# A decoder block on one core: sums of h2 from stored fp32 blocks with grouped plain tiles, and the second MLP product in passes (2,4), (3,5), (1,6), 7

## The chip, the core and the metric

The kernel runs on one core of a Trainium2 chip. Its time is device time in microseconds (us) for one execution. The engines are TensorE (PE; PEld are its weight loads), VectorE (DVE), ScalarE (ACT), GpSimd (POOL) and SyncE (SP, which here only issues DMAs). Each engine works through its own instructions in the order in which they stand in its queue. Names as L1018 are lines of the kernel before.

## The reference

The block has sequence 1024, width 1024 and one layer, all in fp32: a normalisation, two kinds of attention with a gated merge, an output projection, and then the MLP and a last normalisation. The change lies in this last part:

```
h2 = rmsnorm(x, g_norm2) * (1 + scale2) + shift2
x  = x + gate2 * (square(relu(h2 @ w_mlp1)) @ w_mlp2)     # 1024 x 4096, then 4096 x 1024
return rmsnorm(x, g_final)
```

## The kernel before

**Precision.** Every fp32 operand of a matmul is split into a high half (an fp32r copy, by ScalarE) and a low half (the operand less the high half, mostly by VectorE), and a product takes three matmuls: high x high, high x low, low x high.

**h2.** The output projection's rows are normalised into `xn2` (L813), transposed by TensorE into banks (L824), scaled by ScalarE into an fp32 tile `hf2` (L826, a ring of three), and split by VectorE and GpSimd into the `big` tiles `h2[g]` (L828, L829): g is the half of the sequence, k the block of 128 channels.

**First product.** It gives 32 tiles f of 128 hidden units, for two halves of the sequence. Tiles 0 to 3 are plain (`plain_tiles`, L882: 24 matmuls for each tile and half); the other 28 go in 14 pairs through a seven-product scheme of the Strassen-Winograd kind (`pair`, L928, `prod`, L915: 12 matmuls each). The scheme needs four combinations of h2's quarters, T1 to T4 (`combos`, L892), which are made from the split halves between plain tiles 0, 1 and plain tiles 2, 3 (L971). `finish` (L846) applies relu and square and keeps tiles ("hold", "cc") until the four members of a group J of four tiles are there; GpSimd then makes the sums that a second, Strassen, scheme needs on its left side, and they are stored to DRAM as `U_d[1]` to `U_d[7]`.

**Second product.** It runs over eight J (512 hidden units each) in four passes: the Strassen products (2,6), (3,5), (1,4) and 7. In a pass of two, eight banks of PSUM hold 4 tiles of each product, and a unit of 24 matmuls adds one J to four banks (`accumulate`, L1022). A unit's operands are prepared by `operands` (L1013): a block of U_d and one of `w_mlp2`, or a sum of two of its blocks made by GpSimd (L1033), are loaded through the ring `raw` (L995, the first seven in memory of the weight pools, then 20 buffers), and ScalarE and VectorE split them into one of four tiles `ut` of 16 KB a partition. After each pass the banks are added into 16 tiles `C` (rows r, columns c, t). In pass 7 the first four J come bank after bank, the last four J finish one bank at a time.

**The end.** In pass 7 all rows are finished (L1121): x is loaded from `X_d`, C is multiplied by the gate (`g2b`, L1126), GpSimd adds (L1127), ScalarE squares with a sum (L1103), and `output` (L1105) makes the reciprocal root, the scalings and the stores.

**Memory and order.** Memory is a stack of pools on each side; tiles of a pool lie one behind the other in the order in which they are first asked for, and a tile waits for what lay there before. Left of the second product's pools lie only constants and weight buffers (32 KB); above these lay the 64 KB of `big` tiles. The order on each engine is set by a planner that simulates the program: of the instructions that are ready, the one that stands first in the program goes first; semaphores are added afterwards.

## Time and profile before

| | us |
|---|---|
| median of 3 runs | 1708.5 (1706.05 to 1708.88) |
| the profiled execution | 1707.44 |
| its span | 1705.6 |
| TensorE busy | 1592.6 (93%) |
| VectorE busy | 1179.3 (69%) |
| ScalarE busy | 958.0 (56%) |
| GpSimd busy | 736.0 (43%) |
| mean granted TensorE clock | 0.963 |

The span runs from the first to the last instruction that the profile shows. Busy shares are means over the whole span; stages differ. Matmuls are pipelined, so that their shown durations overlap: the pace of a stage is its length over its matmuls.

### The profile page before, as it was taken

Reading aid. Unit: us, or ns where it says so; the run is one execution under the profiler, and the core shown is the slowest. Engines: PE = TensorE matmul, PEld = TensorE weight load, DVE = VectorE, ACT = ScalarE, POOL = GpSimd, SP = SyncE. Lnnn points to the kernel's source line nnn. Section 1 sums busy time; section 2 is a strip of 40 time slices with the busy share of each in tenths; the row PEclk is TensorE's granted clock in tenths of the full one; section 3 lists DMA queues with packets and bytes.
Section 4 is the critical chain, followed back from the end, with each engine's and each line's share of the span. In section 5 each row is a group of like instructions: output and inputs, shape, how many; then the busy total and the mean of one; then the engine's idle time right before and its main releaser. Section 6 shows DMA issues by size and latency. Waiting matters only on the chain. (4 is left out here: it accounts for less than half of the span.)

```text
span 1705.6 us, 22762 instructions
## 1 busy us (share of the span) xinstructions
PE 1592.6 (93%) x7585; PEld 1315.8 (77%) x7585; DVE 1179.3 (69%) x2271; ACT 958.0 (56%) x1678; POOL 736.0 (43%) x611
## 2 busy tenths in 40 slices
PE   5989999998989999999999998699999889999986
PEld 3768787787778888888887887488888668888875
DVE  6786999989945556566767358866555377658478
ACT  4466897896666777666742154355445343434343
POOL 3421112131114565666532117776667543245472
PEclk8999999998999999999999999799999989999998
DMA  9221122121323444545956331254344597566832
GB/s 303 73 47 57 42 72 60 50 71 44 91 51 101 124 128 107 162 146 152 337 175 234 119 116 50 93 167 161 136 153 144 191 364 247 195 239 213 278 100 99
DMA packets 215997, 242.53 MB, mean 142 GB/s; under 512 B 48432, under 2 KB 133504, under 8 KB 215880
## 3 DMA queue, kind: packets, MB, share of 16 engines
q1 hardware_dynamic: 208968, 226.39, 42.3%
q10 hardware_dynamic: 6912, 14.68, 2.2%
q8 instruction: 60, 0.98, 0.2%
q14 instruction: 57, 0.47, 0.1%
HBM read 180.19 MB, written 60.84 MB: 141 GB/s over the span
## 5 line engine op out<-in xcount | busy, mean ns | idle before, releaser
L75 PE MATMUL g<-h_hi,whi 128*128 128x512 f32 x656 | 267.5, 408 | 8.2 <-DVE KA L313 5.8
L75 PE MATMUL g<-h_hi,wlo 128*128 128x512 f32 x656 | 264.9, 404 | 0.0
L75 PE MATMUL g<-h_lo,whi 128*128 128x512 f32 x656 | 263.8, 402 | 0.0
L117 POOL TENSOR_TENSOR wlo<-st,whi 128x1024 fp32r<-128x1024 f32 x56 | 136.9, 2446 | 292.4 <-ACT whi L116 227.9
L1019 DVE TENSOR_TENSOR ut<-rw,ut 128x1024 fp32r<-128x1024 f32 x112 | 186.3, 1706 | 96.5 <-ACT ut L1018 96.5
L1018 ACT ACTIVATE ut<-rw 128x1024 fp32r<-128x1024 f32 x112 | 112.1, 1052 | 154.3 <-PE pv L75 71.5
L1033 POOL TENSOR_TENSOR rw<-rw 128x1024 f32<-128x1024 f32 x40 | 107.9, 2697 | 152.0 <-DMA rw<-in_w_mlp_dram 139.5
L75 PEld LDWEIGHTS g<-h_hi,whi 128*128 128x128 f32 x656 | 126.7, 193 | 34.3 <-DVE KA L313 3.6
L75 PEld LDWEIGHTS g<-h_hi,wlo 128*128 128x128 f32 x656 | 126.2, 192 | 25.0
L75 PEld LDWEIGHTS g<-h_lo,whi 128*128 128x128 f32 x656 | 126.6, 193 | 23.9
L75 PE MATMUL S<-ut 128*128 128x512 f32 (+1 forms) x576 | 139.1, 387 | 4.9 <-DVE C L1074 4.9
L75 PEld LDWEIGHTS S<-ut 128*128 128x128 f32 x576 | 107.8, 193 | 27.0 <-DVE C L1074 5.3
L572 ACT ACTIVATE ph<-ptr 128x512 fp32r<-128x512 f32 (+1 forms) x160 | 86.1, 551 | 56.8 <-PE ptr L571 52.7
L573 DVE TENSOR_TENSOR pl<-ptr,ph 128x512 fp32r<-128x512 f32 (+1 forms) x160 | 99.5, 630 | 26.4 <-ACT ph L572 22.6
L75 PE MATMUL g<-ut 128*128 128x512 f32 (+1 forms) x384 | 96.8, 389 | 20.5 <-ACT ut L1018 12.8
L116 ACT ACTIVATE whi<-st 128x1024 fp32r<-128x1024 f32 x72 | 75.8, 1053 | 71.1 <-PE g L75 23.1
L555 ACT ACTIVATE sp<-sp,mn 128x128 f32<-128x128 f32 (+7 forms) x128 | 98.5, 771 | 28.8 <-DVE mn L551 28.5
L486 DVE TENSOR_SCALAR_CACHE_REDUCE bjunk<-sel_all,cand 128x384 bf16<-128x384 int16 (+7 forms) x132 | 106.5, 806 | 1.4
L558 ACT ACTIVATE sp<-sp,mn 128x128 f32<-128x128 f32 (+7 forms) x128 | 96.8, 770 | 18.7 <-DVE mn L557 18.2
L571 PE MATMUL ptr<-ident,sp 128*128 128x128 f32 x576 | 91.8, 276 | 9.6 <-DVE pl L573 9.6
L75 PEld LDWEIGHTS g<-ut 128*128 128x128 f32 x384 | 71.5, 195 | 35.8 <-ACT ut L1018 13.2
L75 PE MATMUL pv<-ph,V 128*128 128x256 f32 x320 | 87.3, 292 | 1.6 <-DVE yt L580 0.9
(420 smaller groups left out, 3975.5 us busy)
## 6 DMA issues: line engine op xcount, KB each, us to landing
...
```

The source lines that it names most:

```text
L75: nc.tensor.matmul(o, l, r, start=start, stop=stop)
L116: nc.scalar.activation(hi, st, AF.Copy)
L117: (lo_eng or nc.vector).tensor_tensor(lo, st, hi.bitcast(F32), op=ALU.subtract)
L486: nc.vector.tensor_scalar(bjunk[:, :(i + 1) * P], sel[i].bitcast(dt), thr[:, q], None, op0=ALU.is_ge, op1=ALU.add, accum_out=cnt[:, q])
L555: nc.scalar.activation(sp[:, :W], sp[:, :W], AF.Exp, bias=mn[:, len(cs) - 1:len(cs)], scale=-1.0, accum_out=mn[:, 2:3])
L558: nc.scalar.activation(sp[:, :W], sp[:, :W], AF.Copy, scale=mn[:, 3:4])
L571: nc.tensor.transpose(tr[:, n * P:(n + 1) * P], pt[s][:, kb * P:(kb + 1) * P], ident)
L572: nc.scalar.activation(ph[:, z:], tr[:, z:], AF.Copy)
L573: nc.vector.tensor_tensor(pl[:, z:], tr[:, z:], ph[:, z:].bitcast(F32), op=ALU.subtract)
L1018: nc.scalar.activation(ut[:, n], t, AF.Copy)
L1019: nc.vector.tensor_tensor(ut[:, n + 1], t, ut[:, n].bitcast(F32), op=ALU.subtract)
L1033: nc.gpsimd.tensor_tensor(o, a, b, op=op)
```

## The change

Each `hf2` block is also stored in DRAM (`H_d`), its low half is always made by VectorE, and the ring has four tiles. All four plain tiles are one group, first half before second half of the sequence for all four; the weights of tiles 2 and 3 lie in the memory of T4. The holds of group 0 lie in the rings "u" and "cc". T1 to T4 are made after that in the program from the stored fp32 blocks, loaded back through SP: one VectorE difference each, then the split; T4's split comes last. The four `ut` tiles get a pool of their own that is made before all others of the second product. The passes are (2,4), (3,5), (1,6), 7, so that C of rows 4 to 7, columns 0 is final after the first and C of rows 0 to 3, columns 1 after the second; their residuals (`residual`) are made in J = 1 to 4 of the next pass. In pass 7 VectorE makes all residual sums; the outputs of rows 4 to 7 are stored by SP, those of rows 0 to 3 by ScalarE and SP.

```
+H_d = drm.tile([2, KT, P, 512], F32, name="H_d")
...
-                        hf2 = pO.tile([P, 512], F32, name="hf2", tag="hf2", bufs=3)
+                        hf2 = pO.tile([P, 512], F32, name="hf2", tag="hf2", bufs=4)
                         nc.scalar.activation(hf2, tp, AF.Identity, scale=ab[:, 2, k:k + 1], bias=ab[:, 3, k:k + 1])
                         hh, hl = [h2[g][v][k // 4][:, k % 4, :] for v in range(2)]
                         nc.vector.tensor_copy(hh, hf2)
-                        (nc.gpsimd if k % 2 else nc.vector).tensor_tensor(hl, hf2, hh.bitcast(F32), op=ALU.subtract)
+                        nc.vector.tensor_tensor(hl, hf2, hh.bitcast(F32), op=ALU.subtract)
+                        nc.sync.dma_start(H_d[g, k], hf2)
...
-        if g == 0:
-            if J == 0:
-                cc = pM.tile([P, 512], F32, name="hold", tag="sc", bufs=14)
-            else:
-                if "hold" not in grp:
-                    grp["hold"] = big.tile([P, 4, 512], F32, name="hold", tag=("big1h0", "big1l0")[J % 2])
-                cc = grp["hold"][:, 2 * i + half, :]
+        if J == 0 and half == 0:
+            cc = pM.tile([P, 512], F32, name="hold", tag="u", bufs=5)
+        elif J and g == 0:
+            if "hold" not in grp:
+                grp["hold"] = big.tile([P, 4, 512], F32, name="hold", tag=("big1h0", "big1l0")[J % 2])
+            cc = grp["hold"][:, 2 * i + half, :]
...
     def plain_tiles(fs):
-        ws = [split_w([(0, P, w1v[:, :, f * P:(f + 1) * P])], nc.gpsimd if f < 2 else None) for f in fs]
+        ws = []
+        for f in fs:
+            dst = None
+            if f >= 2:
+                t4 = Tm[4][f - 2].rearrange("p a b -> p (a b)")
+                dst = t4[:, 0:1024], t4[:, 1024:2048]
+            ws.append(split_w([(0, P, w1v[:, :, f * P:(f + 1) * P])], nc.gpsimd, dst=dst))
         for half in range(2):
             for f, (hi, lo) in zip(fs, ws):
...
-    def combos(k):
-        def comb(dst, hi_a, hi_b, lo_a, lo_b):
...
+    def put_T(n, k, t):
+        h, l = [v[:, k, :] for v in Tm[n]]
+        nc.scalar.activation(h, t, AF.Copy)
+        nc.vector.tensor_tensor(l, t, h.bitcast(F32), op=ALU.subtract)
+    def combos():
+        t4 = []
+        for k in range(4):
+            f = {}
+            for g, q in ((0, k), (1, k), (1, 4 + k), (0, 4 + k)):
+                f[g, q // 4] = pM.tile([P, 512], F32, name="hc", tag="sc", bufs=14)
+                nc.sync.dma_start(f[g, q // 4], H_d[g, q])
+            b11, b21, b12, b22 = f[0, 0], f[0, 1], f[1, 0], f[1, 1]
+            for o, a, b, n in ((b11, b12, b11, 1), (b12, b22, b12, 3), (b22, b22, b11, 2), (b21, b21, b22, 4)):
+                nc.vector.tensor_tensor(o, a, b, op=ALU.subtract)
+                if n < 4:
+                    put_T(n, k, o)
+            t4.append(b21)
+        for k in range(4):
+            put_T(4, k, t4[k])
...
-    for f in range(0, FP, 2):
-        plain_tiles((f, f + 1))
-        if f == 0:
-            for k in range(4):
-                combos(k)
+    plain_tiles(range(FP))
+    combos()
...
+    pU = pool(st5, "pU")
+    for u in range(4):
+        pU.tile([P, 4, 2, 512], F32R, name="ut", tag=f"ut{u}")
...
-        ut = pN.tile([P, 4, 2, 512], F32R, name="ut", tag=f"ut{u}")
+        ut = pU.tile([P, 4, 2, 512], F32R, name="ut", tag=f"ut{u}")
...
-    def step_26(J):
-        A2, B11, A6, B12 = A(2, J), B(J, 0, 0), A(6, J), B(J, 0, 1)
-        sums(B12, B11, B12, ALU.add)
-        return operands(A2, B11), operands(A6, B12)
+    def step_24(J):
+        A2, B11, A4, B21 = A(2, J), B(J, 0, 0), A(4, J), B(J, 1, 0)
+        u2 = operands(A2, B11)
+        return u2, operands(A4, sums(B21, B21, B11, ALU.subtract))
...
-    def step_14(J):
-        A1, B22, B11, B21, A4 = A(1, J), B(J, 1, 1), B(J, 0, 0), B(J, 1, 0), A(4, J)
+    def step_16(J):
+        A1, B22, B11, A6, B12 = A(1, J), B(J, 1, 1), B(J, 0, 0), A(6, J), B(J, 0, 1)
         sums(B22, B22, B11, ALU.add)
-        u1 = operands(A1, B22)
-        sums(B11, B21, B11, ALU.subtract)
-        return u1, operands(A4, B11)
+        sums(B12, B11, B12, ALU.add)
+        return operands(A1, B22), operands(A6, B12)
...
-    def run(step):
+    def run(step, what=None):
         ps = banks(8)
         for J in range(NJ):
             for p, ut in enumerate(step(J)):
                 for tau in range(4):
                     accumulate(ps[4 * p + tau], ut, tau, J == 0, J == NJ - 1)
+            if what and 1 <= J <= 4:
+                what(J - 1)
         return ps
...
     def cadd(key, ps, op=ALU.add):
-        nc.vector.tensor_tensor(C[key], ps, C[key], op=op)
-    ps = run(step_26)
+        o = C[key]
+        nc.vector.tensor_tensor(o, *((o, ps) if op == ALU.subtract else (ps, o)), op=op)
+    def square(t, src, n):
+        w = src.shape[-1]
+        nc.scalar.activation(sqj[:, 0:w], src, AF.Square, accum_out=ss3[:, t, n:n + 1])
+    def residual(r, c, t):
+        xt = raw().rearrange("p a b -> p (a b)")[:, 0:512]
+        nc.sync.dma_start(xt, X_d[4 * r + t][:, H[c]])
+        c_ = C[r, c, t]
+        nc.vector.tensor_tensor(c_, c_, g2b[:, H[c]], op=ALU.mult)
+        nc.vector.tensor_tensor(c_, c_, xt, op=ALU.add)
+        square(4 * r + t, c_, 1 - c)
+    ps = run(step_24)
+    nc.sync.dma_start(g2b, bass.AP(tensor=R_d.tensor, offset=R_d.offset + D, ap=[[0, P], [1, D]]))
+    nc.sync.dma_start(gfb, bass.AP(tensor=g_final.tensor, offset=g_final.offset, ap=[[0, P], [1, D]]))
     for t in range(4):
         nc.scalar.activation(C[1, 0, t], ps[t], AF.Copy)
+        nc.vector.tensor_scalar(C[1, 1, t], ps[t], -1.0, None, op0=ALU.mult)
     for t in range(4):
-        nc.vector.tensor_tensor(C[1, 1, t], ps[4 + t], C[1, 0, t], op=ALU.subtract)
-    ps = run(step_35)
+        nc.scalar.activation(C[0, 0, t], ps[4 + t], AF.Copy)
+        cadd((1, 0, t), ps[4 + t])
+    ps = run(step_35, lambda n: residual(1, 0, n))
     for t in range(4):
         nc.scalar.activation(C[0, 1, t], ps[t], AF.Copy)
         cadd((1, 1, t), ps[t])
     for t in range(4):
-        nc.scalar.activation(C[0, 0, t], ps[4 + t], AF.Copy, scale=-1.0)
         cadd((0, 1, t), ps[4 + t])
-    nc.sync.dma_start(g2b, bass.AP(tensor=R_d.tensor, offset=R_d.offset + D, ap=[[0, P], [1, D]]))
-    nc.sync.dma_start(gfb, bass.AP(tensor=g_final.tensor, offset=g_final.offset, ap=[[0, P], [1, D]]))
-    ps = run(step_14)
+        cadd((0, 0, t), ps[4 + t], ALU.subtract)
+    def right_half(t):
+        residual(0, 1, t)
+        nc.gpsimd.tensor_tensor(C[0, 1, t], C[0, 1, t], gfb[:, H[1]], op=ALU.mult)
+    ps = run(step_16, right_half)
     for t in range(4):
         cadd((1, 1, t), ps[t])
         cadd((0, 0, t), ps[t])
     for t in range(4):
-        cadd((1, 0, t), ps[4 + t])
-        cadd((0, 0, t), ps[4 + t])
...
+        cadd((1, 1, t), ps[4 + t])
+    def rstd(t, nparts):
         nc.vector.tensor_reduce(ss3[:, t, 3:4], ss3[:, t, 0:nparts], axis=mybir.AxisListType.X, op=ALU.add)
-        rs = newton_rstd(pN, ss3[:, t, 3:4], 1, "c", 2)
-        nc.vector.scalar_tensor_tensor(x2[t][:, H[0]], x2[t][:, H[0]], rs, gfb[:, H[0]], op0=ALU.mult, op1=ALU.mult)
-        nc.gpsimd.tensor_tensor(x2[t][:, H[1]], x2[t][:, H[1]], gfb[:, H[1]], op=ALU.mult)
-        nc.scalar.activation(x2[t][:, H[1]], x2[t][:, H[1]], AF.Copy, scale=rs)
-        nc.scalar.dma_start(outr[t * P:(t + 1) * P, H[1]], x2[t][:, H[1]])
-        nc.sync.dma_start(outr[t * P:(t + 1) * P, H[0]], x2[t][:, H[0]])
+        return newton_rstd(pN, ss3[:, t, 3:4], 1, "c", 2)
+    def output(t, c, eng):
+        eng.dma_start(outr[t * P:(t + 1) * P, H[c]], C[t // 4, c, t % 4])
...
-    for t in (0, 1, 2, 3, 4, 5, 6, 7):
-        x2[t] = raw().rearrange("p a b -> p (a b)")
-        nc.sync.dma_start(x2[t], X_d[t])
-        for c in (1, 0):
-            c_ = C[t // 4, c, t % 4]
-            nc.vector.tensor_tensor(c_, c_, g2b[:, H[c]], op=ALU.mult)
-            nc.gpsimd.tensor_tensor(x2[t][:, H[c]], x2[t][:, H[c]], c_, op=ALU.add)
-            if t >= 4 or c == 1:
-                square(t, H[c], 1 - c)
-        if t >= 4:
-            output(t, 2)
+    xh = []
+    for t in range(4):
+        xh.append(raw().rearrange("p a b -> p (a b)")[:, 0:512])
+        nc.sync.dma_start(xh[t], X_d[t][:, H[0]])
+    for t in range(4):
+        residual(1, 1, t)
+        rs = rstd(4 + t, 2)
+        for c in range(2):
+            nc.vector.scalar_tensor_tensor(C[1, c, t], C[1, c, t], rs, gfb[:, H[c]], op0=ALU.mult, op1=ALU.mult)
+            output(4 + t, c, nc.sync)
     for p, (tau, cs) in zip(ps, cols):
         for n, ut in enumerate(units):
             accumulate(p, ut, tau, False, n == len(units) - 1, cs)
         c_ = C[0, 0, tau]
-        nc.vector.tensor_tensor(c_[:, cs], p, g2b[:, cs], op=ALU.mult)
-        nc.vector.tensor_tensor(x2[tau][:, cs], x2[tau][:, cs], c_[:, cs], op=ALU.add)
-        square(tau, cs, 1 if cs.start == 0 else 2)
+        if cs.start == 0:
+            nc.vector.tensor_tensor(c_, c_, g2b[:, H[0]], op=ALU.mult)
+            nc.vector.tensor_tensor(c_, c_, xh[tau], op=ALU.add)
+        pg2 = pN.tile([P, 512], F32, name="pg2", tag="pg2", bufs=2)[:, cs]
+        nc.vector.tensor_tensor(pg2, p, g2b[:, cs], op=ALU.mult)
+        nc.vector.tensor_tensor(c_[:, cs], pg2, c_[:, cs], op=ALU.add)
+        square(tau, c_[:, cs], 1 if cs.start == 0 else 2)
         if cs.stop == 512:
-            output(tau, 2 if cs.start == 0 else 3)
+            rs = rstd(tau, 2 if cs.start == 0 else 3)
+            nc.scalar.activation(C[0, 1, tau], C[0, 1, tau], AF.Copy, scale=rs)
+            output(tau, 1, nc.scalar)
+            nc.vector.scalar_tensor_tensor(c_, c_, rs, gfb[:, H[0]], op0=ALU.mult, op1=ALU.mult)
+            output(tau, 0, nc.sync)
```

## Rows read from the trace of the kernel before

**Rows 1.** table of stretches: stretch, length, busy PE, PEld, DVE, ACT, POOL, clock, DMA, GB/s

```profile
1012.60:1045.00 32.40, 30.98 (x150) 24.92 (x149) 19.06 (x44) 20.12 (x34) 11.50 (x8) 1.00 0.15 51
1045.00:1105.00 60.00, 41.88 (x148) 32.06 (x147) 58.52 (x47) 21.67 (x36) 48.18 (x30) 0.80 0.23 79
1105.00:1345.00 240.00, 240.00 (x1051) 196.97 (x1050) 140.67 (x166) 118.42 (x189) 165.38 (x114) 1.00 0.47 158
1345.00:1375.00 30.00, 17.17 (x67) 13.63 (x66) 9.31 (x10) 11.08 (x15) 13.11 (x9) 0.77 0.57 197
1375.00:1634.20 259.20, 259.20 (x1144) 214.59 (x1143) 170.84 (x114) 101.74 (x113) 111.41 (x44) 1.00 0.73 253
1634.20:1697.40 63.20, 50.55 (x241) 41.99 (x239) 59.25 (x104) 26.92 (x52) 32.92 (x19) 0.86 0.20 69
```

**Rows 2.** timeline of TensorE near the end: start us, us, engine, line, operation

```profile
1691.44 3.04 PE L75 MATMUL g<-ut 128*128 128x256 f32 x24
1694.31 3.04 PE L75 MATMUL S<-ut 128*128 128x256 f32 x24
```

**Rows 3.** waits of TensorE, 1045 to 1105 us: total us, times, longest

```profile
PE tr L75 <- ACT sc L946: 10.2, 1, 10.2
```

**Rows 4.** timeline between the two products (start us, us), [idle before <-releaser]

```profile
1325.50 0.42 SPq L1004 DMA_DIRECT2D rw<-U_d  x1
...
1344.04 0.39 PE L75 MATMUL tr<-big,wlo 128*128 128x512 f32 x1
...
1355.27 2.93 PE L75 MATMUL S<-big,sc 128*128 128x512 f32 x12
...
1366.67 0.32 SPq L865 DMA_DIRECT2D U_d<-hold  x1
...
1367.09 0.38 SPq L1004 DMA_DIRECT2D rw<-in_w_mlp_dram  x1
...
1368.97 7.69 ACT L1018 ACTIVATE ut<-rw 128x1024 fp32r<-128x1024 f32 x8 [8.66 <-DMA U_d<-hold]
...
1371.03 0.79 PE L75 MATMUL g<-ut 128*128 128x512 f32 x1 [12.83 <-ACT ut L1018]
```

**Rows 5.** waits of TensorE, 1630 to 1700 us

```profile
PE g L75 <- DVE ut L1019: 7.7, 2, 6.2
PE S L75 <- DVE C L1074: 4.9, 1, 4.9
```

**Rows 6.** waits of ScalarE, 1610 to 1680 us

```profile
ACT sqj L1103 <- POOL rw L1127: 27.6, 7, 11.3
```

**Rows 7.** instructions on tile tf: ns min/median/max, first to last start us

```profile
L896 POOL TENSOR_TENSOR tf<-big x8: 1287/1732/1751, 1036.6 to 1091.1; 128x512 f32<-128x512 f32 x8
...
L901 DVE TENSOR_TENSOR tf<-tf,te x8: 678/1756/1784, 1041.0 to 1096.2; 128x512 f32<-128x512 f32 x8
```

**Rows 8.** timeline of place A: first plain matmul, last hf2, first product on T2

```profile
1012.84 0.61 PE L75 MATMUL g<-big,whi 128*128 128x512 f32 x2
...
1033.14 0.78 ACT L826 ACTIVATE hf<-pv,ab 128x512 f32<-128x512 f32 x1 [1.16 <-PE pv L824]
...
1096.91 0.79 PE L75 MATMUL tr<-T2h,sc 128*128 128x512 f32 x1 [10.20 <-ACT sc L946]
```

**Rows 9.** instructions on tile ut

```profile
L1018 ACT ACTIVATE ut<-rw x112: 1038/1049/1069, 1369.0 to 1672.8; 128x1024 fp32r<-128x1024 f32 x112
L1019 DVE TENSOR_TENSOR ut<-rw,ut x112: 1208/1226/3431, 1370.1 to 1679.1; 128x1024 fp32r<-128x1024 f32 x112
```

**Rows 10.** costliest groups of the page: busy us, mean ns | idle before

```profile
L1033 POOL TENSOR_TENSOR rw<-rw 128x1024 f32<-128x1024 f32 x40 | 107.9, 2697 | 152.0 <-DMA rw<-in_w_mlp_dram 139.5
```

**Rows 11.** groups of VectorE by form, 1634.2 to 1705.6 us: busy us, mean ns

```profile
L1019 DVE TENSOR_TENSOR ut<-rw,ut 128x1024 fp32r<-128x1024 f32 x14 | 23.7, 1714 | 1.7 <-ACT ut L1018 1.7
L1108 DVE SCALAR_TENSOR_TENSOR rw<-rw,rsc,gfb 128x512 f32<-128x512 f32 x8 | 5.9, 748 | 0.2
L134 DVE RECIPROCAL rsc<-rsc 128x1 f32<-128x1 f32 x8 | 1.2, 159 | 1.0 <-ACT rsc L133 0.9
```

More of the change, by code (lines that the diff above doesn't have):

```diff
@@ L890, in plain_tiles @@
                     finish(ps, f, half)
-        def combos(k):
-            def comb(dst, hi_a, hi_b, lo_a, lo_b):
-                h, l = [t[:, k, :] for t in dst]
-                t = pM.tile([P, 512], F32, name="tf", tag="sc", bufs=14)
-                nc.gpsimd.tensor_tensor(t, hi_a, hi_b, op=ALU.subtract)
-                e = lo_a
-                if lo_b is not None:
-                    e = pM.tile([P, 512], F32, name="te", tag="sc", bufs=14)
-                    nc.vector.tensor_tensor(e, lo_a, lo_b, op=ALU.subtract)
-                nc.vector.tensor_tensor(t, t, e, op=ALU.add)
-                nc.scalar.activation(h, t, AF.Copy)
-                nc.vector.tensor_tensor(l, t, h.bitcast(F32), op=ALU.subtract)
-                return t
-            f = lambda b: [t[:, k, :].bitcast(F32) for t in b]
-            b11, b12, b21, b22 = f(B11), f(B12), f(B21), f(B22)
-            t1 = comb(Tm[1], b12[0], b11[0], b12[1], b11[1])
-            t2 = comb(Tm[2], b22[0], t1, b22[1], None)
-            comb(Tm[3], b22[0], b12[0], b22[1], b12[1])
-            comb(Tm[4], b21[0], t2, b21[1], None)
+        def put_T(n, k, t):
[17 more added lines that the diff above has]
+                put_T(4, k, t4[k])
         turn = [0]
@@ L1071, in block_kernel @@
         ss3 = pN.tile([P, NTT, 4], F32, name="ss3")
+        sqj = pN.tile([P, 512], BF16, name="sqj")
         def cadd(key, ps, op=ALU.add):
-            nc.vector.tensor_tensor(C[key], ps, C[key], op=op)
-        ps = run(step_26)
+            o = C[key]
[13 more added lines that the diff above has]
+        nc.sync.dma_start(gfb, bass.AP(tensor=g_final.tensor, offset=g_final.offset, ap=[[0, P], [1, D]]))
         for t in range(4):
             nc.scalar.activation(C[1, 0, t], ps[t], AF.Copy)
+            nc.vector.tensor_scalar(C[1, 1, t], ps[t], -1.0, None, op0=ALU.mult)
         for t in range(4):
-            nc.vector.tensor_tensor(C[1, 1, t], ps[4 + t], C[1, 0, t], op=ALU.subtract)
-        ps = run(step_35)
+            nc.scalar.activation(C[0, 0, t], ps[4 + t], AF.Copy)
+            cadd((1, 0, t), ps[4 + t])
+        ps = run(step_35, lambda n: residual(1, 0, n))
         for t in range(4):
@@ L1094, in block_kernel @@
         for t in range(4):
-            cadd((1, 0, t), ps[4 + t])
-            cadd((0, 0, t), ps[4 + t])
-        sqj = pN.tile([P, 512], BF16, name="sqj")
-        x2 = {}
-        def square(t, h, n):
-            nc.scalar.activation(sqj[:, 0:h.stop - h.start], x2[t][:, h], AF.Square, accum_out=ss3[:, t, n:n + 1])
-        def output(t, nparts):
-            nc.vector.tensor_reduce(ss3[:, t, 3:4], ss3[:, t, 0:nparts], axis=mybir.AxisListType.X, op=ALU.add)
-            rs = newton_rstd(pN, ss3[:, t, 3:4], 1, "c", 2)
-            nc.vector.scalar_tensor_tensor(x2[t][:, H[0]], x2[t][:, H[0]], rs, gfb[:, H[0]], op0=ALU.mult, op1=ALU.mult)
-            nc.gpsimd.tensor_tensor(x2[t][:, H[1]], x2[t][:, H[1]], gfb[:, H[1]], op=ALU.mult)
-            nc.scalar.activation(x2[t][:, H[1]], x2[t][:, H[1]], AF.Copy, scale=rs)
-            nc.scalar.dma_start(outr[t * P:(t + 1) * P, H[1]], x2[t][:, H[1]])
-            nc.sync.dma_start(outr[t * P:(t + 1) * P, H[0]], x2[t][:, H[0]])
+            cadd((1, 1, t), ps[4 + t])
+        def rstd(t, nparts):
+            nc.vector.tensor_reduce(ss3[:, t, 3:4], ss3[:, t, 0:nparts], axis=mybir.AxisListType.X, op=ALU.add)
+            return newton_rstd(pN, ss3[:, t, 3:4], 1, "c", 2)
+        def output(t, c, eng):
+            eng.dma_start(outr[t * P:(t + 1) * P, H[c]], C[t // 4, c, t % 4])
         cols = [(0, slice(0, 512)), (1, slice(0, 512)), (2, slice(0, 512)), (3, slice(0, 256)), (3, slice(256, 512))]
```

## The prediction

> **What bounds the kernel now.** I read the table of stretches first [rows 1]. TensorE sets the pace wherever it is fed: from 1105 to 1345 us and from 1375 to 1634.2 us its busy time equals the stretch, at a granted clock of 1.00, so that a 512-column matmul costs 240/1051 = 0.2284 us in the first product and 259.2/1144 = 0.2266 us in the second. Three stretches lie outside this. From 1045 to 1105 only 148 matmuls ran, worth 148 x 0.2284 = 33.8 of 60 us: 26.2 us lost. From 1345 to 1375, 67 ran, worth 15.3 of 30 us: 14.7 lost. In the last pass 145 matmuls of 512 columns and 96 of 256 ran; 24 of the narrow ones take 1694.31 - 1691.44 = 2.87 us [rows 2], 0.1196 each, so the stage is worth 32.9 + 11.5 = 44.4 of 63.2 us: 18.8 lost. Together 59.7 us; the change touches just these three places. No matmul is added or taken away (192 plain, 14 pairs of 84, 56 units of 24).
>
> I then asked of each place which wait ends last. Place A, the plain products and the combinations T1 to T4: TensorE sat 10.2 us before the first product on T2 [rows 3], and VectorE was busy for 58.5 of the 60 us [rows 1], so the ScalarE copy named there was late because VectorE was. Place B, between the products: TensorE sat 12.8 us until the first operand copy, which waited for the last U_d store [rows 4]. Place C, the last pass: 4.9 us until a bank was evicted and 7.7 us until operand halves [rows 5]; 18.8 - 12.6 = 6.2 us are the lower clock (0.86) and start-up. Behind C stands ScalarE, held in its queue 27.6 us by squares waiting for GpSimd's adds [rows 6].
>
> **Part A: combinations from stored fp32 blocks, four plain tiles in one group.** Removed: per k, ten VectorE operations (two te, four sums, four low halves) and four GpSimd differences, 40 and 16 in all. Added: per k, four VectorE differences and four low halves, 32 in all, no GpSimd, 16 stores and 16 loads. A VectorE operation of this size takes 0.68 us alone and 1.76 us (median) beside GpSimd, which takes 1.29 us alone [rows 7]; the case to price is how many are met.
>
> When is T2 needed? Plain work starts at 1012.84 [rows 8]. Of the 150 matmuls up to 1045 [rows 1], 32 are transposes, so those cost 30.98 - 118 x 0.2266 = 4.2 us. All four tiles need 192 x 0.2266 = 43.5, so plain ends at 1060.5. The five products that need no T (60 x 0.2284 = 13.7) reach to 1074.2; the last quarter of T2 is read 9 matmuls later, at 1076.3. When is it there? The last hf2 ends at 1033.9 [rows 8]. Store and load cost 2.3 us each, by the step from the last store's issue to the copy that waited for it, 1366.67 to 1368.97 [rows 4]: 1038.5. VectorE then owes 27 operations of k = 0..3 before T2 is whole, five pair halves, and two weight halves of 1.23: 32 x 0.68 + 2.5 = 24.3. GpSimd runs beside it the ten group operations of the first four tiles and four pair sums; each holds one VectorE operation up by 1.76 - 0.68 = 1.08: 15.1. T2 is whole at 1077.9, 1.6 us late. I take 3 us left over for order and clock, nearest to this sum. Bounds: all 34 operations at the contended price (32 x 1.76 + 3.5 = 59.8) put it at 1098, no gain; nothing late gains 26. A loss would need T2 later than now, which eight VectorE and 16 GpSimd operations fewer exclude unless the loads are late (below). A gains 23 (0 to 26).
>
> The rows say that GpSimd's presence costs VectorE 1.08 us an operation. The Trainium skill (SBUF — State Buffer, Who interferes with whom) has the pair of ports as an exclusive lock: a VectorE instruction with two SBUF inputs blocks for all of a GpSimd instruction that started first. Read so, the group operations that stay cost their whole 1.29 us, 14 x 1.29 = 18.1 instead of 15.1; T2 would be 3 us later and the total 1663 by it.
>
> What A costs elsewhere: eight low halves of h2 move from GpSimd to VectorE, 8 x 0.68 = 5.4 us, beside TensorE work (VectorE is busy 19 of 32.4 us there [rows 1]); if h2's second half were late by that, 5.4 us. The hf2 ring now waits for its store: 0.78 [rows 8], about 0.4 for the split and 2.3 over four buffers is one block in 0.9 us, 7 us for eight, while TensorE has the first half's four tiles, 96 x 0.2266 = 21.8 us, to do; nothing. The 32 DMAs take about 0.35 us of issue each on SP, 11 us, where DMA engines are 0.15 busy [rows 1]; behind a load that waits stand the pairs' weights and the U_d stores, and if the sums began 10 us late, A would lose those 10. T4 holds the weights of tiles 2 and 3, so its copies wait for the last plain product, with ScalarE's pair halves behind them; T4 is needed last of the four, and I put nothing.
>
> **Part B: the operand ring in its own pool, made first.** Before, the ring lies behind C, g2b and gfb, so that its first tile covers the hold of the last group, which is free only when its store has landed [rows 4]. Now the four tiles lie exactly over the 64 KB of h2: the first two over its first half, last read by the product that ends about 1344.4 [rows 4], the third ends its wait with the last product, 1358.2, and only the fourth covers the last hold. The first four blocks are issued by 1325.5 [rows 4], so units 0 and 1 (four copies of 1.05, four halves of 1.23 [rows 9]) are ready near 1351 and cover 48 x 0.2266 = 10.9 us from 1358.2. Unit 2 is ready near 1362, needed at 1369. Unit 3 waits for the hold (1369.0) and for a weight block that SP issues behind the last store, at 1367.1 [rows 4]; landed by 1370, its sum 2.7 [rows 10], copy 1.05 and half 1.23: 1375, needed at 1374.5. I leave 1.7 us: B gains 13 (0 if SP's order keeps the early blocks behind the stores too; 14.7 at most). Pairing 4 with 2 instead of 6 with 2 keeps one sum and four blocks per J.
>
> **Part C: three quarters of the output finished in other passes.** C10 is final after (2,4), C01 after (3,5), so their residuals, 16 VectorE operations (10.9 us), and one extra eviction of each of four banks (2.7) fall into 1375 to 1634, where VectorE is busy 170.8 of 259.2 us [rows 1]: hidden, and worth up to 13.6 if that cover fails. GpSimd's 16 adds and eight multiplies shrink to four multiplies, so ScalarE's squares wait for VectorE only. Cost of VectorE from the last pass's start: 12 operand halves (units 2 to 7) 12 x 1.23 = 14.7; at 0.68 each, five evictions 3.4 and 16 residual operations 10.9; 12 scalings of 0.75 [rows 11] 9.0; eight rows of seven small operations of 0.16 [rows 11] 9.0; ten last sums, six at 0.68 and four of half the width at about 0.43, 5.8. That is 52.8 us, against 44.4 of matmuls and 8.2 of tail after them (1697.4 to 1705.6): VectorE is as long as TensorE, with no slack. So I leave 4.8 us for its gaps: C gains 14. Bounds: if its operations stay at today's contended mean (1.71 for halves [rows 11]), about 12 x 0.48 = 5.8 us more, and a blocked ScalarE gives all of 18.8 back; nothing late gains 18.8.
>
> **Sum.** 23 + 13 + 14 = 50, less 2 us for stalls at the new pass boundaries (bounds 0 and 13.6, above; nearest to the two boundaries inside the full stretch, which cost nothing) is 48. The span 1705.6 becomes 1657.6, with the 1.8 us around it 1659.4; the profiled execution, 1707.4, is 1.1 below the median 1708.5: 1660.5, forecast 1660.
>
> **Rivals.** (1) VectorE stays the wall in place A, by late loads or GpSimd at every step: A gains 8, time 1675. For it: 58.5 of 60 us busy; against: 8 fewer operations and 16 fewer GpSimd ones. (2) The ring gains nothing, the early blocks being queued behind the stores: B gains 2, time 1671. Against: SP issued the first four before 1326. (3) The last pass is VectorE's: C gains 3, time 1671. For it: the 52.8 us above. (4) Slower: the squares of the eight early residuals hold ScalarE in its queue as they do in place C [rows 6], now inside full passes. One such wait was 11.3 us there; two units prepared ahead cover 10.9 us, but after the first the cover isn't rebuilt at once. At 7 us each TensorE loses 56 and the time is 1716; it decides from (1708.5 - 1660)/8 = 6.1 us each. Against: those waits were for GpSimd and for a load at the end of the ring; these blocks are fetched a ring ahead.
>
> **Chances.** Forecast 0.60 (own range 1648 to 1669), (1) 0.14, (2) 0.08, (3) 0.12, (4) 0.04, several of (1) to (3) together without a gain 0.02. The floor is 1708.5 - 59.7 = 1649, and 1646 with the 2.5 us by which the lowest run lies under the median; the top takes in two rivals at once. Faster by over 0.2% (about what this kernel's measurement can tell) 0.94, within it 0.02, slower 0.04.
>
> **What would show it.** Right: a first T2 product near 1077 with VectorE operations mostly at 0.68; full TensorE rate from about 1358 less A's gain; no ScalarE square waiting for GpSimd; matmuls ending 8 us before the span. Wrong: a wait on H_d loads before T1, a unit waiting for a U_d store, VectorE at full in the last pass with TensorE waiting on ut, or squares that hold ut copies in passes (3,5) and (1,6).

## The result and the profile after

The changed kernel takes **1659.3 us** (median of 4 runs, 1657.1 to 1664.1), the kernel before on the same chip 1707.3: ratio **0.973 [0.970, 0.976]**, 48 us less. The forecast was 1660. The profiled execution took 1664.1 us, 4.8 above the median. Its span, 1662.3 us, is 43.3 shorter than that of [rows 1].

From here on a line number is one of the kernel whose profile is shown. The table of stretches of the changed kernel, cut at its own events: first plain matmul, 1045, first product on T2, end of the first product, full rate again, pass 7, and the tail behind the matmuls (columns as in [rows 1]).

```profile
1014.73:1045.00 30.27, 26.04 (x120) 20.57 (x119) 18.67 (x50) 19.13 (x32) 5.45 (x2) 0.94 0.58 210
1045.00:1083.12 38.12, 38.12 (x167) 31.07 (x166) 31.49 (x36) 21.87 (x37) 27.98 (x15) 1.00 0.44 142
1083.12:1338.60 255.48, 255.48 (x1117) 209.35 (x1115) 143.13 (x171) 122.70 (x195) 169.98 (x117) 1.00 0.47 159
1338.60:1368.00 29.40, 23.43 (x89) 18.62 (x89) 22.46 (x15) 15.02 (x16) 16.92 (x10) 0.83 0.77 277
1368.00:1610.13 242.13, 241.95 (x1066) 199.66 (x1065) 179.03 (x134) 99.86 (x116) 113.67 (x41) 1.00 0.75 257
1610.13:1654.50 44.37, 44.37 (x241) 38.48 (x239) 40.94 (x98) 18.66 (x36) 0.00 (x0) 1.00 0.23 83
...
1654.50:1662.30 7.80, 0.02 (x1) 0.00 (x0) 2.70 (x10) 1.44 (x4) 0.00 (x0) 0.78 0.36 134
```

- **A**, first plain matmul to the end of the first product: 1338.60 - 1014.73 = 323.9 us. Before, 1355.27 + 2.93 - 1012.84 = 345.4 [rows 4, 8]. Gain 21.5.
- **B**, from there to pass 7: 1610.13 - 1338.60 = 271.5. Before, 1634.2 - 1358.2 = 276.0. Gain 4.5.
- **C**, pass 7 to its last matmul: 44.4 against 63.2 [rows 1], gain 18.8; the tail is 7.8 instead of 8.2, 0.4.
- Plain work began 1014.73 - 1012.84 = 1.9 us later. In the profiled executions of the runs below it began between 1004.9 and 1014.0, though the kernels e1 to e12 hardly differ ahead of it; so the stretches behind it are compared, not the spans.

21.5 + 4.5 + 18.8 + 0.4 - 1.9 = 43.3, the whole difference.

TensorE's waits, 1005 to 1400 us, answering to [rows 3] and the first wait of [rows 4]:

```profile
PE g L75 <- ACT ut L1025: 4.6, 1, 4.6
PE S L75 <- ACT T4h L117: 3.3, 1, 3.3
PE g L75 <- DVE ut L1026: 1.4, 1, 1.4
PE tr L825 <- ACT hf L827: 0.7, 1, 0.7
```

From 1590 on, where [rows 5] had 12.6 us, none is left. The wall of place A is gone: the instructions on the stored blocks (tile hc, ns min/median/max, first to last start), answering to [rows 7]:

```profile
L913 DVE TENSOR_TENSOR hc<-hc x16: 678/681/2951, 1037.7 to 1055.9; 128x512 f32<-128x512 f32 x16
...
L902 DVE TENSOR_TENSOR T2l<-hc,T2h x4: 677/679/682, 1044.5 to 1056.6; 128x512 fp32r<-128x512 f32 x4
...
L901 ACT ACTIVATE T4h<-hc x4: 615/616/621, 1067.1 to 1069.2; 128x512 fp32r<-128x512 f32 x4
```

T2 is whole at 1057.2, 26 us before TensorE asks for it. One difference took 2.95 us, the first: it started beside a GpSimd half. The other way round, GpSimd's first sum began while VectorE worked through this row without a gap, and took 6.32 us, until the row had ended (GpSimd's timeline: start us, us):

```profile
1037.71 2.41 POOL L118 TENSOR_TENSOR T4l<-st,T4l 128x1024 fp32r<-128x1024 f32 x1
1052.07 6.32 POOL L948 TENSOR_TENSOR S<-st 128x512 f32<-128x512 f32 x1 [11.95 <-issue]
```

### The profile page after: what moved, and what is told of

Read it like the earlier page. It is cut to its first block, busy times and chain, and to the rows that moved or that the text cites. A ratio compares the mean times of both kernels' runs of the same rounds, so it can differ in the third digit from the quotient of the medians.

```text
span 1662.3 us, 22793 instructions
## 1 busy us (share of the span) xinstructions
PE 1582.9 (95%) x7585; PEld 1310.5 (79%) x7585; DVE 1155.4 (70%) x2293; ACT 955.7 (57%) x1674; POOL 684.4 (41%) x569
## 4 chain that ended last, share of the span: by engine, by line
PE 74%; DVE 14%; ACT 4%; DMA 4%; issue 3%; POOL 1%; SPq 1%; DVEq 0%; ACTq 0%; POOLq 0%
PE g L75 33%; PE S L75 23%; PE tr L75 8%; PE pv L75 7%; DVE bjunk L487 3%; PE ptr L572 2%; DVE acc L247 1%; DMA gt<-G_d 1%; DVE pl L574 1%; DVE sp L552 1%; DMA wap<-in_w_ada_dram 1%; ACT eqt L484 1%; ACT sp L556 1%; DVE gt L777 1%; ACT sp L559 1%
## 5 line engine op out<-in xcount | busy, mean ns | idle before, releaser
L1026 DVE TENSOR_TENSOR ut<-rw,ut 128x1024 fp32r<-128x1024 f32 x112 | 179.0, 1644 | 69.5 <-ACT ut L1025 69.5
L1025 ACT ACTIVATE ut<-rw 128x1024 fp32r<-128x1024 f32 x112 | 112.0, 1052 | 144.9 <-PE pv L75 66.5
L1040 POOL TENSOR_TENSOR rw<-rw 128x1024 f32<-128x1024 f32 x40 | 115.6, 2893 | 127.3 <-DMA rw<-in_w_mlp_dram 110.0
L75 PEld LDWEIGHTS S<-ut 128*128 128x128 f32 x576 | 106.5, 190 | 21.5 <-DVE ut L1026 0.4
L559 ACT ACTIVATE sp<-sp,mn 128x128 f32<-128x128 f32 (+7 forms) x128 | 96.8, 770 | 17.2 <-DVE mn L558 16.7
```

The costliest lines, as they stand in the source:

```text
L75: nc.tensor.matmul(o, l, r, start=start, stop=stop)
L559: nc.scalar.activation(sp[:, :W], sp[:, :W], AF.Copy, scale=mn[:, 3:4])
L1025: nc.scalar.activation(ut[:, n], t, AF.Copy)
L1026: nc.vector.tensor_tensor(ut[:, n + 1], t, ut[:, n].bitcast(F32), op=ALU.subtract)
L1040: nc.gpsimd.tensor_tensor(o, a, b, op=op)
```

## The experiments

Each kernel is the changed one with the edit shown. "A" is the stretch above, "rest" runs from the end of the first product to the end of the span. Both come from the profiled execution; a kernel that leaves a stretch as it is repeats A within 323.9 to 325.3 and the rest within 322.1 to 323.7.

| run | us | ratio to before | A | rest |
|---|---|---|---|---|
| before | 1705 to 1708 | 1 | 345.4 | 347.4 |
| changed | 1659.3 | 0.973 [0.970, 0.976] | 323.9 | 323.7 |
| e1 again | 1660.3 | 0.973 [0.971, 0.975] | 324.1 | 323.7 |
| e2 ring back | 1665.1 | 0.976 [0.974, 0.978] | 324.9 | 328.5 |
| e3 first units | 1653.1 | 0.969 [0.967, 0.971] | 324.1 | 314.3 |
| e4 old passes | 1677.5 | 0.983 [0.981, 0.985] | 325.1 | 338.8 |
| e5 sums only | 1663.7 | 0.976 [0.972, 0.979] | 329.0 | 322.1 |
| e6 group only | 1683.3 | 0.987 [0.984, 0.989] | 348.1 | 323.5 |
| e7 differences on GpSimd | 1668.4 | 0.978 [0.975, 0.980] | 333.1 | 322.8 |
| e8 adds on GpSimd | 1659.4 | 0.972 [0.970, 0.975] | 325.1 | 323.1 |
| e9 late residuals | 1668.1 | 0.977 [0.974, 0.979] | 325.3 | 328.0 |
| e10 two groups | 1664.9 | 0.977 [0.975, 0.978] | 330.1 | 322.7 |
| e11 both | 1654.3 | 0.970 [0.968, 0.971] | 329.9 | 313.4 |
| e12 sums on VectorE | 1651.0 | 0.967 [0.964, 0.969] | 325.7 | 313.5 |

**e1.** The base.

> The changed kernel once more, unaltered, as the base for the runs beside it. Every theory expects 1657 to 1664 us and a ratio to the kernel before of 0.970 to 0.976.

1660.3 us; both stretches within 0.2.

### Place A

**e5, e6: the two halves of part A.**

```
-        plain_tiles(range(FP))
+        plain_tiles((0, 1))
         combos()
+        plain_tiles((2, 3))      # e5, weights in the weight ring; e6 keeps one group
...                               # and takes combos(k) of the kernel before
```

> The combinations come from the stored fp32 blocks as in the changed kernel, but the plain tiles stand as before: two before the combinations and two behind, each with weights from the weight ring. Theory: what counts is that VectorE's differences run at 0.68 us and have little GpSimd work beside them; TensorE then has 31 us of plain work as cover instead of 61, so T2, whole some 43 us after the first plain matmul, is late by about 12 us, while the copies into T4's place and their 3.3 us wait fall away: 1665 to 1672 us. Rival: the grouping is what counts and the sums alone bring nothing, so the first product is as before and the time 1681 us. Second rival: the sums alone bring all, 1659 us or less.

> The plain tiles are grouped with the weights of tiles 2 and 3 in T4's place, but the combinations are made from the split halves as in the kernel before (a GpSimd difference of the high halves, VectorE differences of the low halves and an add). Theory: VectorE's work per block is twice as much and stands beside GpSimd (1.76 us instead of 0.68), so T2 is whole some 20 us later than TensorE's four plain tiles end, at about 1097, and 15 to 25 us of the first product's 21.5 us gain are lost: 1674 to 1684 us. Rival: the grouped plain tiles cover the old combinations too, and the sums bring nothing more: 1659 to 1663 us.

e5: A is 329.0, 16.4 us below before. e6: 348.1, 2.8 above it. So the stored sums carry the gain; the grouping adds 329.0 - 323.9 = 5.1 with them and costs 2.8 without. e5's time fell just under its expected 1665 because T2 was not late by 12 us: its first product stood 68.3 us behind the first plain matmul, as in the changed kernel (68.4). The 5.1 us that it lacks lie behind that: TensorE waits 4.0 us, until 1098.75, for a finish on VectorE, the one that e10 below explains. e6's time lies in its range, but T2 is whole by 1091.5 and TensorE asks for it only at 1106.6; what it waits for before that are pair halves (`sc`, 7.7 and 3.5 us) and a copy out of a bank (4.5). e6's combinations (groups by line, 1030 to 1105 us: busy us, mean ns) run at the contended price, as before:

```profile
L908 DVE TENSOR_TENSOR tf<-tf,te 128x512 f32<-128x512 f32 x8 | 12.9, 1611 | 0.1
...
L910 DVE TENSOR_TENSOR T1l<-tf,T1h 128x512 fp32r<-128x512 f32 x4 | 6.7, 1687 | 0.2
```

**e7: the differences beside VectorE.**

```
-                    nc.vector.tensor_tensor(o, a, b, op=ALU.subtract)
+                    nc.gpsimd.tensor_tensor(o, a, b, op=ALU.subtract)
```

> The 16 differences of the stored blocks run on GpSimd instead of VectorE, beside VectorE's low halves. Theory: contention, which the prediction counted at 15 us and the trace of the changed kernel did not show, appears here: a GpSimd difference 1.3 us, the VectorE low half beside it up to 1.76 instead of 0.68 us; T2 is whole at 1070 to 1080 instead of 1057, still ahead of TensorE's 1076 or just behind it, so 0 to 4 us slower than the changed kernel, 1659 to 1663 us. Rival: GpSimd stands in a longer queue here (group operations and weight copies), T2 is whole after 1085, and the time is 1668 us or more.

Both sides missed part: 1668.4 us, A 9.2 longer. T2 is whole at 1071.0 + 1.7 = 1072.7, inside the theory's 1070 to 1080, and TensorE asks for it only at 1090.8. What TensorE waits for, 5.0 us, is a pair half (`sc`) that stands in VectorE's queue behind two slow T4 halves. Tile hc, and the timelines of GpSimd and VectorE:

```profile
L913 POOL TENSOR_TENSOR hc<-hc x16: 1275/1733/2266, 1038.5 to 1073.9; 128x512 f32<-128x512 f32 x16
...
L902 DVE TENSOR_TENSOR T2l<-hc,T2h x4: 1546/1670/1789, 1047.7 to 1071.0; 128x512 fp32r<-128x512 f32 x4
...
1070.44 1.75 POOL L948 TENSOR_TENSOR S<-st,S 128x512 f32<-128x512 f32 x1
...
1070.96 1.79 DVE L902 TENSOR_TENSOR T2l<-hc,T2h 128x512 fp32r<-128x512 f32 x1
...
1076.06 3.42 DVE L902 TENSOR_TENSOR T4l<-hc,T4h 128x512 fp32r<-128x512 f32 x2
1079.41 0.68 DVE L954 TENSOR_TENSOR sc<-S,sc 128x512 fp32r<-128x512 f32 x1
```

Contention costs T2's low halves 1.67 us instead of 0.68; the changed kernel avoids most of it, as GpSimd has little work beside the combinations there.

**e10: the 3.3 us.** In the changed kernel the copies of tile 2's weights stand in ScalarE's queue behind the last hf2 (ScalarE's timeline: start us, us):

```profile
1032.87 0.78 ACT L827 ACTIVATE hf<-pv,ab 128x512 f32<-128x512 f32 x1 [0.80 <-DVE big L830]
1033.55 1.05 ACT L117 ACTIVATE T4h<-st 128x1024 fp32r<-128x1024 f32 x1
1034.50 1.05 ACT L117 ACTIVATE T4l<-st 128x1024 fp32r<-128x1024 f32 x1
```

```
-        plain_tiles(range(FP))
+        plain_tiles((0, 1))
+        plain_tiles((2, 3))
         combos()
```

> The four plain tiles run as two groups of two (tiles 0 and 1 over both halves of h2, then tiles 2 and 3), still with the weights of tiles 2 and 3 in T4's place and the combinations behind; nothing else differs. The weights of tile 2 are then needed 31 us after the first plain matmul instead of 15, at about 1045 and not at 1031. Theory: the 3.3 us that TensorE waits for these weights, and the low clock (0.89) behind it, come from the order of the tiles; both go, so 4 to 7 us faster than the changed kernel, 1653 to 1656 us. Rival: the second half of h2 is now needed at 1028, before its last blocks are written (the last hf2 ends near 1034), and the wait only changes its name: 1659 to 1663 us. Second rival: T2 comes no earlier, and TensorE waits later for T2 or for a block of products what it won here: 1658 to 1660 us.

The wait went, as the theory had it, and T2's first product moved from 68.4 to 64.8 us behind the first plain matmul. Then TensorE lost more than that: A is 6.2 longer, 1664.9 us, worse than even the second rival. TensorE's waits, then the chain behind the longest, from its end, e10:

```profile
PE g L75 <- DVE hold L862: 7.0, 1, 7.0
```

```profile
1092.01 2.26 DVE L118 TENSOR_TENSOR wlo<-st,whi 128x1024 fp32r<-128x1024 f32 x1 [3.97 <-ACT whi L117]
...
1095.50 0.69 DVE L862 TENSOR_TENSOR hold<-g,u 128x512 f32<-128x512 f32 x1
...
1090.92 1.06 ACT L117 ACTIVATE whi<-st 128x1024 fp32r<-128x1024 f32 x1 [4.29 <-DMA st<-in_w_mlp_dram]
...
1086.86 0.38 SPq L940 DMA_DIRECT2D st<-in_w_mlp_dram  x1
...
1086.14 0.69 DVE L954 TENSOR_TENSOR sc<-st,sc 128x512 fp32r<-128x512 f32 x1 [1.28 <-ACT sc L953]
...
1084.29 0.63 ACT L863 ACTIVATE cc<-cc 128x512 f32<-128x512 f32 x1 [3.03 <-DVE cc L862]
...
1085.50 0.61 ACT L953 ACTIVATE sc<-st 128x512 fp32r<-128x512 f32 x1
```

Read from the end: the finish that frees TensorE's bank (1095.50) stands behind the low half of the fourth pair's weights; that waits for their high half, and this for a load. The load is issued at 1086.86, when VectorE's split of the second pair's second raw block (1086.14) has released the slot; ScalarE's part of that split (1085.50) stands in its queue behind an operation that waits 3.0 us for a finish on VectorE. Further back in the same queue ScalarE waits 3.7 us for GpSimd's sums of the second pair, which stand between the group operations of the plain tiles. The load is issued 78.5 us behind the first plain matmul; in the changed kernel it is 1089.91 - 1014.73 = 75.2. Even so the same finish had only 0.7 us of slack there: it ended near 1098.4 and TensorE took the bank at 1099.16. What TensorE wins ahead of this point it loses here again, unless the chain comes earlier too.

### Place B

**e2: the ring alone.**

```
-        pU = pool(st5, "pU")
-        for u in range(4):
-            pU.tile([P, 4, 2, 512], F32R, name="ut", tag=f"ut{u}")
         pN = pool(st5, "pN")
...
-            ut = pU.tile([P, 4, 2, 512], F32R, name="ut", tag=f"ut{u}")
+            ut = pN.tile([P, 4, 2, 512], F32R, name="ut", tag=f"ut{u}")
```

> The second product's operand ring goes back into the pool that holds the raw blocks and scratch; all else is as in the changed kernel. Theory: the comparison of the two traces gives the stretch from the end of the first product to pass 7 only 4.5 us less than before, so without the ring's own pool the kernel is about 4.5 us slower than the changed one, 1664 us (bounds 1662 to 1667). Rival, the prediction's term: the ring's own pool is worth 13 us, so 1672 us. Second rival: the ring is worth nothing, and the 4.5 us came with the other passes, so 1659 us.

The theory held: 4.8 us slower, the rest 4.8 longer, and the wait of [rows 4] is back at 12.8 us. The ring's own pool is worth 4.8, not 13.

**e3: why not 13.** ScalarE in the changed kernel between the products (last column: idle before):

```profile
1333.90 0.63 ACT L863 ACTIVATE cc<-cc 128x512 f32<-128x512 f32 x1 [6.86 <-DVE cc L862]
...
1339.42 0.63 ACT L863 ACTIVATE cc<-cc 128x512 f32<-128x512 f32 x1 [1.48 <-DVE cc L862]
1340.08 0.63 ACT L864 ACTIVATE cc<-cc 128x512 f32<-128x512 f32 x1
1340.74 0.33 ACTq L866 DMA_DIRECT2D U_d<-cc  x1
1341.11 5.79 ACT L1025 ACTIVATE ut<-rw 128x1024 fp32r<-128x1024 f32 x6 [0.40 <-ACT cc L864]
1352.17 1.07 ACT L1025 ACTIVATE ut<-rw 128x1024 fp32r<-128x1024 f32 x1 [5.26 <-DMA U_d<-hold]
```

ScalarE stands idle for 6.9 us before 1333.90, yet the first copy starts at 1341.11, right behind the last finish, and that finish can only follow the last product. No copy into the new pool stands ahead of the last instruction of the pools closed before it; why the planner sets it so, no run shows. e3 issues the first two units before that close, over h2's first half:

```
+    A2, B11_, A4, B21_ = blocks          # loaded into weight and stage buffers
...
+    nc.gpsimd.tensor_tensor(B21_, B21_, B11_, op=ALU.subtract)
+    for p, ut in enumerate((first_unit(A2, B11_, ("big0h0", "big0h1")),
+                            first_unit(A4, B21_, ("big0l0", "big0l1")))):
...                                       # and their 48 matmuls
     big_stack.close()
```

> The first two units of pass (2,4) are written over the first half of h2 and are issued, with their 24 matmuls a column, before the pools of the first product are closed. Their copies then stand ahead of the last finish in ScalarE's queue, and the second block row's loads ahead of the last stores. Theory: the 4.6 and 1.4 us that TensorE waits for the first operands after the first product, and part of the low clock behind them, come from the queue order on ScalarE (the copies stand behind the last finish, which ends at 1340.74); so 4 to 7 us faster than the changed kernel, 1653 to 1655 us. Rival: the operands wait for the stores and loads of the first product's last tiles, whatever the queue; so no change, 1658 to 1661 us. Second rival: the copies now hold up the last finish and its stores, and the wait moves to the later blocks; 1660 to 1665 us.

7.1 us faster, at the far end of the theory; the rest is 9.4 shorter. TensorE goes from one product to the next without a gap:

```profile
1330.55 2.93 PE L75 MATMUL S<-big,sc 128*128 128x512 f32 x12
1333.32 1.52 PE L75 MATMUL g<-uf 128*128 128x512 f32 x6
```

From 1333.48 to 1368 its clock is 1.00 and 151 matmuls run, where the changed kernel has 89 in 29.4 us at 0.83. The first copy now starts at 1316.80, 16.7 us before the first product ends. The copy that waits 8.2 us for the last store is still there, and TensorE doesn't notice it:

```profile
1316.80 1.06 ACT L994 ACTIVATE uf<-rw 128x1024 fp32r<-128x1024 f32 x1 [0.47 <-PE S L75]
...
1346.28 1.06 ACT L1051 ACTIVATE ut<-rw 128x1024 fp32r<-128x1024 f32 x1 [8.18 <-DMA U_d<-hold]
```

The edit moves loads as well, into other buffers, but SP's next loads come alike: 11.0 us behind the end of the first product here (1344.49), 11.8 in the changed kernel (1350.38).

### Place C

**e4: the passes alone.**

```
-        ps = run(step_35, lambda n: residual(1, 0, n))
...                    # the second product's passes of the kernel before
```

> The changed kernel's first product and ring, with the passes of the kernel before in the second product. Theory, from the comparison of the two traces: the stretch of the last pass gives 18.8 us and its tail 0.4 us, so 19 us slower than the changed kernel, 1678 us. Rival, the prediction's term: 14 us for the passes less 2 us for their boundaries, so 1671 us. Second rival: the passes are worth what TensorE's own waits in the stretch before were, 12.6 us, so 1672 us with no clock won back.

1677.5 us, the theory's 1678, and 17.2 above e1; the rest is 15.1 longer. Both rivals (1671, 1672) fall. The ring is worth 347.4 - 338.8 = 8.6 with the old passes and 4.8 with the new ones. Of the 8.6, 6.2 lie between the first product and pass 7 (276.0 against 269.8) and 3.1 in pass 7 (63.2 against 60.1), less 0.7 in the tail; why pass 7 is shorter there stays open.

**e8, e9: what makes the last pass free.**

```
-            nc.vector.tensor_tensor(c_, c_, xt, op=ALU.add)
+            nc.gpsimd.tensor_tensor(c_, c_, xt, op=ALU.add)      # e8 only
```
```
-        ps = run(step_35, lambda n: residual(1, 0, n))
+        ps = run(step_35)                                         # e9 only
...      # right_half(t), residual(1, 0, t) are issued in pass 7
```

> The add of each residual block goes from VectorE to GpSimd; all else as in the changed kernel. Theory: the squares that follow the adds stand in ScalarE's queue ahead of operand copies, and each add on GpSimd stands behind its sums of blocks; ScalarE waits for GpSimd again and TensorE for operands, 5 to 15 us slower, 1664 to 1674 us. Rival: with the residuals spread over three passes there is room on GpSimd, and nothing reaches TensorE: within 2 us of the changed kernel.

> The residual blocks (1,0) and (0,1), eight of the twelve that the changed kernel finishes during passes (3,5) and (1,6), are issued in pass 7 instead; the passes themselves stay (2,4), (3,5), (1,6), 7. Theory: what frees the last pass is that VectorE has 41 of its 44.4 us there and not more; with eight adds and up to eight multiplications of 0.68 us (5.4 to 10.9 us) more, VectorE ends after TensorE, the operands come late, and the time is 3 to 9 us above the changed kernel, 1663 to 1669 us. Rival: the gain of 17 us lies in the pass that is alone at the end (one sum and one pair of operands per block, all units of its second half made ahead), so that late residuals cost under 2 us: 1659 to 1662 us.

e8's theory fell: the squares do wait for GpSimd again (26.0 us in ten waits), but TensorE waits 0.8 us for operands, and the time is that of the changed kernel. So the move of the adds to VectorE is worth nothing once the residuals are spread; four GpSimd adds are left in pass 7. e9 costs 4 to 8 us (the rest 4.3 longer in its profiled execution, the fastest of five; the medians of e9 and e1, on two chips, 7.9 apart). The time is the theory's, the wait is not: VectorE is busy 49.5 of the 50.2 us of pass 7, but TensorE waits at the head of pass 7 for banks whose eviction stands behind the late residual work in VectorE's queue:

```profile
PE g L75 <- DVE C L1085: 2.0, 1, 2.0
PE S L75 <- DVE C L1085: 1.9, 3, 1.2
```

```profile
1599.78 1.21 DVE L1026 TENSOR_TENSOR ut<-rw,ut 128x1024 fp32r<-128x1024 f32 x1
1600.92 1.28 DVE L1085 TENSOR_TENSOR C<-g,C 128x512 f32<-128x512 f32 x2
1602.12 1.21 DVE L1026 TENSOR_TENSOR ut<-rw,ut 128x1024 fp32r<-128x1024 f32 x1
1603.25 0.68 DVE L1097 TENSOR_TENSOR C<-C,rw 128x512 f32<-128x512 f32 x1
1603.85 1.28 DVE L1085 TENSOR_TENSOR C<-S,C 128x512 f32<-128x512 f32 x2
```

The early residuals are thus a quarter to a half of the 15 to 17 us of e4. For the other part compare pass 7 in e4 and e9, which has the same matmuls in both. In e4 GpSimd runs 18 operations there (32.0 us), VectorE's halves beside them take 1.71 us, and TensorE waits 7.1 us for halves; in e9 GpSimd has none, the halves take 1.21 us, and no such wait is left (groups by form, pass 7, e4 and e9):

```profile
L1026 DVE TENSOR_TENSOR ut<-rw,ut 128x1024 fp32r<-128x1024 f32 x14 | 23.7, 1714 | 1.7 <-ACT ut L1025 1.7
...
L1026 DVE TENSOR_TENSOR ut<-rw,ut 128x1024 fp32r<-128x1024 f32 x14 | 16.8, 1210 | 0.0
```

So the other part goes with GpSimd's adds and multiplications in pass 7; no run takes only these away.

### Together

> The first two units of pass (2,4) over h2's first half and the plain tiles in two groups, together. Theory: the two waits lie 300 us apart and have nothing in common, so the gains add: 7 us from the first and 4 to 7 from the second, 1646 to 1650 us. Rival: the second gains nothing, and the time is that of the first units alone, 1653 us.

1654.3 us: the rival. The 7 us from the first units are there (rest 313.4), the second edit costs its 6 in A (329.9).

**e12.** e11, and

```
-                nc.gpsimd.tensor_tensor(S[:, o, :], a, b, op=op)
+                (nc.vector if f0 == FP + 2 else nc.gpsimd).tensor_tensor(S[:, o, :], a, b, op=op)
```

> Both of the last run, and the four weight sums S of the second pair of the first product go from GpSimd to VectorE. With the plain tiles in two groups TensorE waits 7.0 us for a finish on VectorE that stands behind a low half of weights, whose raw block is loaded only when GpSimd has ended these sums at 1082.51 (they stand between the eight group operations of the plain tiles). VectorE has 6.9 and 4.4 us of idle time there, and its sums take 0.68 us each. Theory: the raw slot comes free some 5 to 7 us earlier, the 7.0 us wait and the low clock behind it go, and the time is 5 to 9 us below the last run, 1645 to 1649 us. Rival: the slot is held by the last split of the raw block (ScalarE and VectorE, to 1086.8), not by the sums, so the wait stays at 5 us or more: 1651 to 1655 us. Second rival: VectorE's sums stand ahead of the finishes that free TensorE's banks and stall it elsewhere: 1655 us or more.

Half of it, and the rival had the cause: the load that the chain waits for is held by the split, not by the sums. The slot of the sums came free 7.7 us earlier (load issued 66.5 us behind the first plain matmul instead of 74.2). The load behind the split was issued at 1084.75, 75.1 us behind instead of 78.5; the block was copied 3.3 us earlier (79.2 instead of 82.5), and the wait fell from 7.0 to 3.6, not the rival's 5 or more:

```profile
1076.11 0.94 SPq L940 DMA_DIRECT2D st<-in_w_mlp_dram  x1
...
1084.75 6.82 SPq L940 DMA_DIRECT2D st<-in_w_mlp_dram  x2
...
1088.85 1.06 ACT L117 ACTIVATE whi<-st 128x1024 fp32r<-128x1024 f32 x1 [4.33 <-DMA st<-in_w_mlp_dram]
...
1094.21 0.50 PE L75 MATMUL g<-T3h,sc 128*128 128x512 f32 x1 [3.62 <-DVE hold L862]
```

From issue to copy it is 4.1 us, as in e10 (4.1) and in the changed kernel (4.2). So the chain now stands where the changed kernel has it (75.2), and TensorE, which comes to T2 3.6 us earlier (64.7 instead of 68.4), waits 3.6. 1651.0 us is the fastest median, and every run of e3, e11 and e12 (1655.6 or less) lies below every run of the changed kernel (1656.5 or more); but e12 and e3 are not told apart (0.967 [0.964, 0.969], 0.969 [0.967, 0.971]), and by A (325.7, 324.1) e12's two extra edits bring nothing over e3.

## Why the prediction came out as it did

The total is right because two mis-sized terms cancel: 23 + 13 + 14 - 2 = 48 was forecast, 21.5 + 4.5 + 18.8 + 0.4 came, less 1.9 of start. That is 43.3, between two profiled executions; the medians lie 48 apart, as the profiled execution of the changed kernel stood 4.8 above its median. To hit 1660 within 1 us was luck.

**A, 23: right in size, wrong in what is left over.** The need was well placed: without loss T2's first product stands 43.5 + 13.7 + 4.2 = 61.4 us behind the first plain matmul. It stood at 68.4. But the supply was not the 1077.9 of the sum. The step that failed is "GpSimd runs beside it ... each holds one VectorE operation up". In the changed kernel GpSimd had no work between 1040.1 and 1052.07, and its first sum was then held by VectorE's row and not the row by it; of the 15.1 us of contention 2.3 arose, at the first difference. The five pair halves and two weight halves (5.9 us) came behind T2, too. So T2 was whole 42.5 us behind the first plain matmul, not 65.1. The price of 1.08 us an operation was right for T2's halves where GpSimd is present (e7: 1.67 - 0.68 = 0.99; longest 1.79), less for T1's (1.10 - 0.68 = 0.42).

The Trainium skill (SBUF — State Buffer, Who interferes with whom) calls the shared pair of ports an exclusive lock. The trace agrees, in both directions: the T2 half that starts at 1070.96 in e7, 0.52 us behind a GpSimd sum (1070.44 to 1072.19), ends 0.56 us behind that sum's end, so it pays what is left of the sum and not all of it; and the sum of 6.32 us in the changed kernel ended 1.2 us behind VectorE's row.

Of the 7.0 us that were lost ahead of T2's first product, 4.3 are waits (3.3 for the weights of tile 2, 1.0 for hf2), and the rest goes with the lower clock (0.94 in the first stretch). The sum put nothing there: I looked at T4's own copies at the end and not at the weight copies at the start, which stand behind the last hf2 in ScalarE's queue. Without that wait (e10) the 68.4 become 64.8. e10 also shows that this loss could not simply be taken back: without it the next chain ends last.

**B, 13: the term that was wrong.** "Units 0 and 1 are ready near 1351", 7 us before the first product ends, took memory and loads for the only conditions. In the changed kernel the first copy starts 1341.11 - 1338.60 = 2.5 us after that end, with its blocks issued by 1325.5; the instruction simply stands behind the last finish. e2 prices the ring at 4.8 us, and e3, which moves the first copies ahead of the finish, gives 9.3 more (271.5 less e3's 262.2). Rival 2 (B gains 2) was nearer to the 4.5 than the forecast's 13, but named another cause, SP's stores; e3 has the same store wait and still won the 9.3.

**C, 14: too small.** The working put VectorE at 52.8 us of work against 52.6 of room. The profile has 40.94 us in the pass and 2.70 in the tail, 43.6. The list of operations was nearly right: added by length, VectorE's groups from 1610 on come to 48.8 us, and the halves, with no GpSimd instruction left in this stage, take 1213 ns, as the sum had it (1.23), and not the 1714 of [rows 11]:

```profile
L1026 DVE TENSOR_TENSOR ut<-rw,ut 128x1024 fp32r<-128x1024 f32 x12 | 14.3, 1213 | 1.1 <-ACT ut L1025 1.1
```

But 0.68 us is an instruction from start to end; one behind the other they start 0.60 apart, and the 108 of them overlap by 48.8 - 43.6 = 5.2 us. Rival 3 had therefore nothing to stand on. The 2 us for the pass boundaries were not needed either: TensorE's waits from 1368 to 1610 sum to 0.2.

**Rival 4** (squares that block ScalarE) can be read off e8: ten squares waited for GpSimd's adds, 26.0 us together and 9.4 at most, and 0.8 us of it reached TensorE, not the 6.1 for each of eight that it needed. In the changed kernel, too, squares held ScalarE during the passes (1368 to 1610 us), for VectorE's adds:

```profile
ACT sqj L1089 <- DVE C L1097: 16.2, 4, 6.4
```

One of these waits, 6.4 us, was longer than the 6.1, but TensorE's waits there sum to 0.2.
